# Value fetches issued behind the query and key fetches, and at the joint of two stages a product drawn forward, two sums per slice on GpSimd and a new order of blocks

## The chip, the cores and the metric

One core of a Trainium2 chip runs the whole kernel; the other cores are idle. The metric is the device time of one execution in microseconds (us), as the median over repeated executions. All data is float32. TensorE (PE in the profile) does the products, ScalarE (ACT) and VectorE (DVE) prepare their operands and take their results, GpSimd (POOL) does some sums and issues DMAs, SyncE (SP) only issues DMAs.

## The reference, cut to what matters

One layer of a bidirectional encoder over 512 tokens of width 1024: a half-step feed-forward, a mixer of two attentions (A and B) with gates, and a second half-step feed-forward.

```python
x = x + 0.5 * swiglu(rmsnorm(x, ffn1_norm), w1, w3, w2)       # FFN a
h = rmsnorm(x, mix_norm)
proj = h @ w_in                                               # A's q, k, v; B's q, k, v; gates
# A: 24 heads of 64 in 3 groups (dilation 1, 4, 16); banded scores with a table of biases,
scores = einsum(q, k) * 64 ** -0.5 + bias                     # masked outside the band
outs = softmax(scores) @ v                                    # groups joined by their log-sum-exp
merged = sigmoid(g_A) * (o_a @ w_branch_a) + sigmoid(g_B) * (o_b @ w_branch_b)
x = x + merged @ w_out
x = x + 0.5 * swiglu(rmsnorm(x, ffn2_norm), ...)              # FFN b
return rmsnorm(x, final_norm)
```

## The kernel before

Activations lie with features on the partitions: `x[0..7]`, eight tiles of 128 features by 512 tokens. Every float32 operand is split into a high part H and a rest L, and every product is three matmuls in a row (`mm3`, lines 256 to 258: H·H, H·L, L·H). A weight tile is fetched raw (`wr`, `wa`, `wt`), ScalarE makes its H (line 241) and VectorE its L (line 242).

PE's order is the order in which the code is written. The other engines' instructions are put in order by the framework, and each engine then works strictly in its order: a waiting instruction holds up all behind it, DMA issues included. DMAs are issued by SP and by GpSimd, each in its own queue.

**The joint of FFN a and the projection.** The last eight products of FFN a run over the rows of `x` in the order `ROWS = (0, 4, 1, 5, 2, 6, 3, 7)`. Behind each, `add` (lines 529 and 530, VectorE) updates `x[d]`, `norm_h` makes `hH[d]` on ScalarE (line 398) and `hL[d]` on VectorE (line 399), and `norm_sq` squares `x[d]` on ScalarE and adds it into `acc` (line 409; five of the adds on GpSimd, two on VectorE). From row pair k, `tq_steps` makes operands of a Strassen product: ScalarE copies the rows scaled into `Traw` (`put`), `sums` forms four sums of 128 x 256 on VectorE (lines 709 to 711), `part` splits them into `TH`, `TL` and `TQ` (line 718). PE's next product is the gate product g0 (`feat`), which takes `hH[k]`, `hL[k]` in the order k = 0..7. Behind it comes the Strassen projection of queries, keys and values (`project_qk`, slices f = 0, 2, .. 14, each of seven products A11, S1, S2, A12, S3, S4, A22 in the order that `slots` gives); for f = 0 the order is A11, A12, S1, ...; the S products read `TH`, `TL`, `TQ`.

**From the projection to the scores.** Finished slices are stored to DRAM by GpSimd: queries and keys to `qk_d` (line 746), values to `v_d` (line 762). `mixer` fetches them back: `fetch(0)` the six `qk` tiles of head pair 0, `fetch_v` the three value tiles `V0`, `V1`, `V2` of 1 MB each, all from GpSimd's queue. One gate product follows on PE (8 steps, `GAP_F`), then the scores of head pair 0 (`scores_a`): per step ("pair") 6 to 12 small matmuls into two PSUM banks (line 850), then two products of another gate block as a filler. VectorE adds the bias tile and takes the maximum (line 855); the bias tiles `W` (one per head) are fetched by SP from `zd`, each in two halves (lines 823 and 824); steps 0 and 1 need the first half only. There are four score banks, so step 2 waits until VectorE has read step 0's. After the four steps ScalarE takes exponentials, and their sums go through DRAM (`d`, lines 871 to 876) and come back in another order; SP then issues the `W` tiles of head pair 1. The tiles `qk` come from a ring of nine.

Of the kernel before, what the change touches and what calls it, by code (L numbers as in the profile page):

```python
# [25 lines left out]
NSW = NSQ + 6  # L26
ROWS = (0, 4, 1, 5, 2, 6, 3, 7)
# [13 lines left out]
NK = 8  # L41
# [28 lines left out]
def f32(t):  # L70
    return t.bitcast(F32)


class Layer:
# [56 lines left out]
    @staticmethod  # L131
    def slots(fs, ahead=False):
        at = {7 * i + 2 * j: (f, step) for i, f in enumerate(fs) for j, step in enumerate(STEPS)}
        if ahead:
            at[1] = at.pop(6)
        return [at[k] for k in sorted(at)]

    def ffn_order(self, s):
# [124 lines left out]
    def aux(self, name):  # L263
        return self.psa.tile([128, T], F32, tag="aux", name=name)

    def feat(self, name, n, done):
        ps = self.bank()
        H, L = self.weights(name, n)
        for k in range(NK):
            s = slice(128 * k, 128 * k + 128)  # L270
            self.mm3(ps, H[:, s], L[:, s], self.hH[k], self.hL[k], k == 0, k == NK - 1)
            if k == NK - 1:
                done(ps)
            yield

# [366 lines left out]
    def stream(self, items, held=None):  # L642
        nc = self.nc
        later = lambda fn: fn if held is None else lambda ps: held.append((fn, ps))
        for kind, n in items:
            if kind == "qk":
                hp, g = PAIRS[n]
                for part in range(2):

                    def done(ps, hp=hp, part=part, g=g):  # L650
                        t = self.qk[hp][part, g] = self.ap.tile([128, T], F32, tag="qk", name="qk", bufs=9)
                        nc.vector.tensor_mul(t.rearrange("p (r m) -> p r m", r=4),
                                             ps.rearrange("p (m r) -> p r m", r=4),
                                             self.acc.rearrange("p (r m) -> p r m", r=4))

                    yield from self.feat("waq", 2 * n + part, done)
            elif kind == "g":

                def done(ps, j=n):
                    z = self.tmp.tile([128, T], F32, tag="t", name="z")  # L660
                    nc.vector.tensor_mul(z, ps, self.R)
                    nc.sync.dma_start(self.gate_d[j], z)

                yield from self.feat("wg", n, later(done))
            elif kind == "pa":
                self.ma = [self.mp.tile([128, T], F32, name=f"ma{d}") for d in range(NK)]
                for d in range(NK):
                    ps = self.bank()
                    for k in range(4):
                        self.mm3(ps, *self.block("wpa", 4 * d + k), self.oH[k], self.oL[k], k == 0, k == 3)  # L670
                        if k == 3:
                            nc.scalar.copy(self.ma[d], ps)
                        yield
            else:
                toks = [(lambda t, i=i: t[:, 128 * i:128 * i + 128]) for i in range(4)]
                yield from self.token("wb", 4 * n, toks, lambda i, b, grp=n: self.rope(grp, i, b))
                self.turn()
            self.past.add((kind, n))

    def fetch(self, hp):  # L680
        for f, (h, g) in enumerate(PAIRS[:NSQ]):
            if h == hp:
                for part in range(2):
                    t = self.qk[hp][part, g] = self.ap.tile([128, T], F32, tag="qk", name="qk", bufs=9)
                    self.nc.gpsimd.dma_start(t, self.qk_d[2 * f + part])

    def fetch_v(self):
        for g in range(3):
            rows = self.v_d[g].rearrange("(m r) f -> m r f", r=4) if g else self.v_d[g].rearrange("(i p) f -> p i f", p=128)
            self.nc.gpsimd.dma_start(self.V[g], rows)  # L690

    def tq_open(self, gp):
# [5 lines left out]
    def tq_steps(self, k):  # L698
        nc = self.nc
        raw = self.cp.tile([128, 1024], F32, tag="c1", name="Traw").rearrange("p (c n) -> p c n", c=4)  # L700

        def put(e):
            d = k + 4 * e
            nc.scalar.activation(raw[:, 1:3] if e else raw[:, 0:4:3], self.x[d].rearrange("p (a n) -> p a n", a=2), AF.Copy,
                                 scale=self.par[:, G_MIX + d:G_MIX + d + 1])

        def sums():
            b = [raw[:, c] for c in (0, 3, 1, 2)]
            neg = lambda o, x, y: nc.vector.scalar_tensor_tensor(o, x, -1.0, y, op0=ALU.mult, op1=ALU.subtract)
            nc.vector.tensor_sub(b[0], b[0], b[1])  # L710
            nc.vector.tensor_sub(b[1], b[3], b[1])
            neg(b[3], b[3], b[0])
            neg(b[2], b[3], b[2])

        def part():
            for src, (H, L) in ((raw[:, 0:3], (self.TH[:, :, k], self.TL[:, :, k])), (raw[:, 3], (t[:, k] for t in self.TQ["S3"]))):
                nc.scalar.copy(H, src)
                nc.vector.tensor_sub(L, src, f32(H))

        return [lambda: put(0), lambda: put(1), sums, part]  # L720

    def project_qk(self, gp):
        nc, cp = self.nc, self.cp
        if True:
# [34 lines left out]

            def store_v(f, at, o):  # L760
                dst = self.v_d[(f - NSQ) // 2].rearrange("(i p) f -> p i f", p=128)
                nc.gpsimd.dma_start(dst[:, :, at:at + 256], o.rearrange("p (i f) -> p i f", i=4))

            def evict(f, step, ps):
                perm = f < NSQ and PAIRS[f][1] > 0
# [299 lines left out]
    def mixer(self):  # L1065
        nc, tc = self.nc, self.tc
# [4 lines left out]
        with tc.tile_pool(name="oA", bufs=1, reuse_waits="tile") as oa:  # L1071
            self.oH = [oa.tile([128, T], F32R, name=f"oH{h}") for h in range(4)]
            self.oL = [oa.tile([128, T], F32R, name=f"oL{h}") for h in range(4)]
            with tc.tile_pool(name="A", bufs=1, reuse_waits="tile") as ap:
                self.ap = ap
                self.V.append(ap.tile([128, 4, 512], F32, name="V2"))
                self.fetch(0)
                self.fetch_v()
                gap = lambda n: [next(fill) for _ in range(n)]
                gap(GAP_F)  # L1080
                held = None
                for hp in range(4):
                    if hp == 3:
                        self.until(fill, ("qk", 11))
                    res = []
                    self.weave(self.scores_a(hp, res), fill)
                    if hp < 3:
                        self.fetch(hp + 1)
                    if held:
                        gap(GAP_Y if hp > 1 else GAP_1)  # L1090
                        self.weave(self.values_a(hp - 1, *held), fill)
                    held = res
                gap(GAP_X)
                self.weave(self.values_a(3, *held), fill)
# [189 lines left out]
```

## Time and profile before

| | |
|---|---|
| time, median of 3 runs | 1277.19 us (1275.91 to 1277.29) |
| the profiled execution | 1272.24 us, of which the span of its instructions is 1270.5 us |
| TensorE busy | 1242.5 us, 98% of the span |
| VectorE, ScalarE, GpSimd busy | 917.2, 605.3, 131.2 us |
| mean granted TensorE clock | 0.992 |

A busy share is an average over the whole span. The times in the text are us from the first instruction of the profiled execution. Of the "joint" the text speaks for 322 to 364 us, of the "scores" for 505 to 560 us.

### The profile page before, as it was taken

The numbers are of one execution on the slowest core, as the hardware profiler recorded it, in microseconds if no ns is written. First come the engines' busy times: TensorE is split into PE (matmuls) and PEld (weight loads), VectorE is DVE, ScalarE is ACT, GpSimd is POOL, SyncE is SP. The second block draws the span as 40 slices with busy tenths as digits, with TensorE's granted clock in tenths as the row PEclk, the third lists the DMA queues.
The fourth block names the chain that finished last, engine by engine and source line by source line (L and its number), as shares of the span: only waits on it lengthen the run. The fifth ranks groups of instructions, "written<-read, shape, count | busy, mean of one in ns | idle before, by whom it ended". The sixth has DMA issues, their size and how long they took to land.

```text
span 1270.5 us, 20497 instructions
## 1 busy us (share of the span) xinstructions
PE 1242.5 (98%) x8214; PEld 1107.6 (87%) x8214; DVE 917.2 (72%) x1372; ACT 605.3 (48%) x903; POOL 131.2 (10%) x139
## 2 busy tenths in 40 slices
PE   9999999999999999699999999999999999999997
PEld 7897999899889999477788878888889989988996
DVE  7784687569988886366746798856777747874775
ACT  8551354155554445354423446655465415532553
POOL 1111110001212110310000200000301000100001
PEclk9999999999999999899999999999999999999998
DMA  9875766367369873853223220147837636743222
GB/s 299 232 187 177 189 187 181 98 168 198 100 147 258 249 200 113 302 168 102 76 104 108 83 92 26 34 142 215 223 101 199 183 94 176 194 150 106 62 82 67
DMA packets 88271, 192.95 MB, mean 152 GB/s; under 512 B 12768, under 2 KB 19312, under 8 KB 87920
## 3 DMA queue, kind: packets, MB, share of 16 engines
q1 hardware_dynamic: 68336, 142.32, 33.5%
q0 software_dynamic: 19120, 48.78, 18.3%
q8 instruction: 64, 1.05, 0.3%
q10 hardware_dynamic: 720, 0.55, 0.1%
q14 instruction: 31, 0.25, 0.1%
HBM read 176.84 MB, written 18.43 MB: 154 GB/s over the span
## 4 chain that ended last, share of the span: by engine, by line
PE 91%; DVE 4%; DMA 2%; issue 1%; ACT 1%; SPq 0%; POOL 0%; POOLq 0%; DVEq 0%
PE mm L256 23%; PE mm L257 22%; PE mm L258 22%; PE Y L257 4%; PE Y L256 4%; PE Y L258 4%; PE X L256 2%; PE X L257 2%; PE X L258 2%; PE S L850 1%; PE mm L901 1%; DMA qk<-qk_d 1%; PE Tb L1040 1%; PE T L919 1%; DVE wl L242 1%
## 5 line engine op out<-in xcount | busy, mean ns | idle before, releaser
L241 ACT CAST wh<-wr 128x1024 fp32r<-128x1024 f32 x133 | 139.4, 1049 | 178.4 <-PE mm L257 126.5
L256 PE MATMUL mm<-hH,wh 128*128 128x256 f32 (+1 forms) x600 | 201.4, 336 | 2.0 <-ACT hH L398 1.9
L257 PE MATMUL mm<-hL,wh 128*128 128x256 f32 (+1 forms) x600 | 196.6, 328 | 1.1 <-DVE hL L399 1.0
L258 PE MATMUL mm<-hH,wl 128*128 128x256 f32 (+1 forms) x600 | 196.4, 327 | 0.9 <-DVE wl L242 0.9
L242 DVE TENSOR_TENSOR wl<-wr,wh 128x1024 fp32r<-128x1024 f32 x133 | 163.0, 1226 | 29.3 <-ACT wh L241 28.9
L256 PE MATMUL mm<-gg,wh 128*128 128x512 f32 (+1 forms) x376 | 141.5, 376 | 0.0
L257 PE MATMUL mm<-gg,wh 128*128 128x512 f32 (+1 forms) x376 | 141.0, 375 | 0.0
L258 PE MATMUL mm<-gg,wl 128*128 128x512 f32 (+1 forms) x376 | 141.0, 375 | 0.0
L256 PEld LDWEIGHTS mm<-hH,wh 128*128 128x128 f32 x600 | 113.4, 189 | 17.9 <-issue 3.7
L257 PEld LDWEIGHTS mm<-hL,wh 128*128 128x128 f32 x600 | 113.6, 189 | 11.6 <-DVE hL L399 2.6
L258 PEld LDWEIGHTS mm<-hH,wl 128*128 128x128 f32 x600 | 113.2, 189 | 11.9 <-DVE wl L242 1.3
L257 PE MATMUL mm<-TL,wh 128*128 128x256 f32 x384 | 106.0, 276 | 0.0
L258 PE MATMUL mm<-TH,wl 128*128 128x256 f32 x384 | 106.0, 276 | 0.0
L256 PE MATMUL mm<-TH,wh 128*128 128x256 f32 x384 | 106.0, 276 | 0.0
L241 ACT CAST wh<-wa 128x1024 fp32r<-128x1024 f32 x54 | 56.8, 1051 | 96.0 <-PE mm L257 48.3
L241 ACT CAST wh<-ws 128x1024 fp32r<-128x1024 f32 x54 | 56.8, 1052 | 76.6 <-PE mm L257 49.2
L242 DVE TENSOR_TENSOR wl<-wt,wh 128x1024 fp32r<-128x1024 f32 x54 | 66.1, 1224 | 34.5 <-ACT wh L241 33.6
L529 DVE TENSOR_TENSOR u<-mm,R 128x512 f32<-128x512 f32 (+1 forms) x52 | 33.7, 648 | 79.2 <-PE mm L258 79.0
L241 ACT CAST wh<-wt 128x1024 fp32r<-128x1024 f32 x54 | 56.8, 1052 | 67.0 <-PE mm L257 39.8
L242 DVE TENSOR_TENSOR wl<-wa,wh 128x1024 fp32r<-128x1024 f32 x54 | 67.0, 1241 | 27.5 <-ACT wh L241 27.5
L256 PEld LDWEIGHTS mm<-gg,wh 128*128 128x128 f32 x376 | 70.6, 188 | 14.1 <-PE mm L258 0.9
L258 PEld LDWEIGHTS mm<-gg,wl 128*128 128x128 f32 x376 | 70.6, 188 | 12.9
(261 smaller groups left out, 3209.2 us busy)
## 6 DMA issues: line engine op xcount, KB each, us to landing
wr<-in_w2a SPq DMA_DIRECT2D x22, 512.0 KB, 3.7
wr<-in_w2b SPq DMA_DIRECT2D x22, 512.0 KB, 3.5
wt<-in_w13b SPq DMA_DIRECT2D x20, 512.0 KB, 4.1
wa<-in_w13b SPq DMA_DIRECT2D x20, 512.0 KB, 3.4
wt<-in_w13b POOLq DMA_DIRECT2D x20, 512.0 KB, 5.8
wt<-in_w13a SPq DMA_DIRECT2D x18, 512.0 KB, 3.5
wt<-in_w13a POOLq DMA_DIRECT2D x18, 512.0 KB, 6.0
wa<-in_w13a SPq DMA_DIRECT2D x18, 512.0 KB, 3.5
```

Of the source, the lines that this page charges most:

```text
L241: self.nc.scalar.copy(H, raw)
L242: self.nc.vector.tensor_sub(L, raw, f32(H))
L256: mm(out, lH, rH, start=start, stop=False, skip_group_check=more)
L257: mm(out, lH, rL, start=False, stop=False, skip_group_check=more)
L258: mm(out, lL, rH, start=False, stop=stop, skip_group_check=more)
L529: nc.vector.tensor_mul(u, ps, R)
L850: nc.tensor.matmul(*args, start=True, stop=True)
L901: nc.tensor.matmul(oc, v, p, start=st, stop=sp)
L919: nc.tensor.transpose(ps[:, 128 * b:128 * b + 128], P[h][:, c0 + 128 * b:c0 + 128 * b + 128], self.ident)
L1040: nc.tensor.transpose(pt[:, 128 * j:128 * j + 128], P[h, j][:, 128 * k:128 * k + 128], self.ident)
```

## The change

It has five parts: (1) `slots(..., ahead=True)` draws the A11 product of slice f = 2 in front of S1 of slice 0; (2) gate products take their blocks in the order `ROWS`; (3) for k = 0, 1, 2 the first two of the four sums of `sums` are made by GpSimd; (4) `fetch_v` is split: `V0` is issued behind the last `qk` fetch of head pair 0, `V1` and `V2` behind the third `qk` fetch of head pair 1; (5) the two value stores of the last slice (f = 14) are issued by SP.

```diff
     def slots(fs, ahead=False):
         at = {7 * i + 2 * j: (f, step) for i, f in enumerate(fs) for j, step in enumerate(STEPS)}
         if ahead:
-            at[1] = at.pop(6)
+            at[1], at[2], at[3] = at.pop(6), at.pop(7), at.pop(2)
...
-    def feat(self, name, n, done):
+    def feat(self, name, n, done, ks=range(NK)):
...
-        for k in range(NK):
+        for k in ks:
...
-                yield from self.feat("wg", n, later(done))
+                yield from self.feat("wg", n, later(done), ROWS)
...
-    def fetch_v(self):
-        for g in range(3):
-            rows = ...
+                    pins.append(self.nc.gpsimd.dma_start(t, self.qk_d[2 * f + part]))
+        return pins
+
+    def fetch_v(self, g, pin):
+        rows = ...
+        with self.tc.issue_after(pin.ins):
             self.nc.gpsimd.dma_start(self.V[g], rows)
...
-            nc.vector.tensor_sub(b[0], b[0], b[1])
-            nc.vector.tensor_sub(b[1], b[3], b[1])
+            eng = nc.gpsimd if k < 3 else nc.vector
+            eng.tensor_sub(b[0], b[0], b[1])
+            eng.tensor_sub(b[1], b[3], b[1])
             neg(b[3], b[3], b[0])
             neg(b[2], b[3], b[2])
...
-                nc.gpsimd.dma_start(dst[:, :, at:at + 256], o.rearrange("p (i f) -> p i f", i=4))
+                (nc.sync if f == NSW - 2 else nc.gpsimd).dma_start(dst[:, :, at:at + 256], ...)
...
-                self.fetch(0)
-                self.fetch_v()
+                self.fetch_v(0, self.fetch(0)[-1])
...
-                    if hp < 3:
-                        self.fetch(hp + 1)
+                    pins = self.fetch(hp + 1) if hp < 3 else []
+                    if hp == 0:
+                        self.fetch_v(1, pins[2])
+                        self.fetch_v(2, pins[2])
```

At the joint, GpSimd's rows in the changed kernel. `Traw_3275`, `Traw_3344` and `Traw_3417` are the sums' tiles of k = 0, 1, 2, and the `sq` tiles are the squares of rows 4, 1, 5, 2, 6:

```order
L409 TENSOR_TENSOR acc_93<-acc_93,sq_3271 128x512
L713 TENSOR_TENSOR Traw_3275<-Traw_3275 128x256
L714 TENSOR_TENSOR Traw_3275<-Traw_3275 128x256
L409 TENSOR_TENSOR acc_93<-acc_93,sq_3314 128x512
L713 TENSOR_TENSOR Traw_3344<-Traw_3344 128x256
L409 TENSOR_TENSOR acc_93<-acc_93,sq_3341 128x512
L714 TENSOR_TENSOR Traw_3344<-Traw_3344 128x256
L409 TENSOR_TENSOR acc_93<-acc_93,sq_3383 128x512
L713 TENSOR_TENSOR Traw_3417<-Traw_3417 128x256
L409 TENSOR_TENSOR acc_93<-acc_93,sq_3414 128x512
L714 TENSOR_TENSOR Traw_3417<-Traw_3417 128x256
```

Before, only the five `acc` rows stood there. The second sum (line 714) of k = 1 and of k = 2 stands behind one more `acc` add.

The same place on VectorE, from the update of row 3 to the update of row 7, before and then in the changed kernel; line 709 before and line 711 after are the two subtractions that read the sums:

```order
L529 TENSOR_TENSOR u_3451<-mm_3428,R_91 128x512
L711 TENSOR_TENSOR Traw_3417<-Traw_3417 128x256
L530 SCALAR_TENSOR_TENSOR x3_77<-u_3451,x3_77 128x512
L709 SCALAR_TENSOR_TENSOR Traw_3417<-Traw_3417 128x256
L718 TENSOR_TENSOR TQ_3274<-Traw_3417,TQ_3274 128x256
L709 SCALAR_TENSOR_TENSOR Traw_3417<-Traw_3417 128x256
L399 SCALAR_TENSOR_TENSOR hL3_108<-x3_77,par_82,hH3_100 128x512
L409 TENSOR_TENSOR acc_93<-acc_93,sq_3456 128x512
L718 TENSOR_TENSOR TL_187<-Traw_3417,TH_186 128x3x256
L529 TENSOR_TENSOR u_3478<-mm_3459,R_91 128x512
```

```order
L529 TENSOR_TENSOR u_3451<-mm_3428,R_91 128x512
L711 SCALAR_TENSOR_TENSOR Traw_3417<-Traw_3417 128x256
L721 TENSOR_TENSOR TQ_3274<-Traw_3417,TQ_3274 128x256
L711 SCALAR_TENSOR_TENSOR Traw_3417<-Traw_3417 128x256
L530 SCALAR_TENSOR_TENSOR x3_77<-u_3451,x3_77 128x512
L721 TENSOR_TENSOR TL_187<-Traw_3417,TH_186 128x3x256
L399 SCALAR_TENSOR_TENSOR hL3_108<-x3_77,par_82,hH3_100 128x512
L409 TENSOR_TENSOR acc_93<-acc_93,sq_3456 128x512
L529 TENSOR_TENSOR u_3478<-mm_3459,R_91 128x512
```

The VectorE sum of k = 2 is gone from here, and the update of `x3` now stands behind three rows that need GpSimd's sum.

Between projection and scores, the rows of GpSimd's queue before and then in the changed kernel. Tiles `qk_5421` to `qk_5431` belong to head pair 0, the others to head pair 1:

```order
L762 DMA v_d_115<-qo_5354 128x4x256
L690 DMA V0_5404<-v_d_115 128x4x512
L762 DMA v_d_115<-qo_5390 128x4x256
L690 DMA V1_5405<-v_d_115 128x2048
L685 DMA qk_5421<-qk_d_114 128x512
L685 DMA qk_5423<-qk_d_114 128x512
L685 DMA qk_5425<-qk_d_114 128x512
L685 DMA qk_5427<-qk_d_114 128x512
L685 DMA qk_5429<-qk_d_114 128x512
L685 DMA qk_5431<-qk_d_114 128x512
L690 DMA V2_5420<-v_d_115 128x2048
L685 DMA qk_5606<-qk_d_114 128x512
```

```order
L686 DMA qk_5429<-qk_d_114 128x512
L686 DMA qk_5431<-qk_d_114 128x512
L692 DMA V0_5404<-v_d_115 128x4x512
L686 DMA qk_5604<-qk_d_114 128x512
L686 DMA qk_5606<-qk_d_114 128x512
L686 DMA qk_5608<-qk_d_114 128x512
L686 DMA qk_5610<-qk_d_114 128x512
L686 DMA qk_5612<-qk_d_114 128x512
L692 DMA V1_5405<-v_d_115 128x2048
L692 DMA V2_5420<-v_d_115 128x2048
L686 DMA qk_5614<-qk_d_114 128x512
```

The six `qk` fetches of head pair 0 now stand directly behind the value store of slice 12, three `qk` fetches of head pair 1 stand behind `V0`, and `V1` and `V2` stand behind `qk_5612`.

SP's queue at the same place, before and then in the changed kernel (`W_5470` and `W_5473` before are `W_5468` and `W_5471` after, the bias tiles of the two heads of head pair 0):

```order
L208 DMA wr_5364<-in_waq 128x1024
L208 DMA wr_5441<-in_waq 128x1024
L662 DMA gate_d_113<-z_5467 128x512
L823 DMA W_5470<-zd_181 128x256
L824 DMA W_5470<-zd_181 128x2x128
L823 DMA W_5473<-zd_181 128x256
L824 DMA W_5473<-zd_181 128x2x128
L208 DMA wr_5500<-in_waq 128x1024
```

```order
L765 DMA v_d_115<-qo_5354 128x4x256
L208 DMA wr_5364<-in_waq 128x1024
L765 DMA v_d_115<-qo_5390 128x4x256
L208 DMA wr_5439<-in_waq 128x1024
L826 DMA W_5468<-zd_181 128x256
L827 DMA W_5468<-zd_181 128x2x128
L662 DMA gate_d_113<-z_5465 128x512
L826 DMA W_5471<-zd_181 128x256
L827 DMA W_5471<-zd_181 128x2x128
L208 DMA wr_5498<-in_waq 128x1024
```

The two value stores came in, the first head's `W` moved ahead of the store of the gate product, and the second head's `W` still stands behind it.

## Rows read from the trace of the kernel before

**Rows 1.** The page: busy time, share of the span and instructions of PE, and the shares by engine of the chain that ended last.
```profile
PE 1242.5 (98%) x8214; PEld 1107.6 (87%) x8214; DVE 917.2 (72%) x1372; ACT 605.3 (48%) x903; POOL 131.2 (10%) x139
PE 91%; DVE 4%; DMA 2%; issue 1%; ACT 1%; SPq 0%; POOL 0%; POOLq 0%; DVEq 0%
```

**Rows 2.** Waits of PE over the whole span: what waited, for what, us in total, times, the longest.
```profile
PE S L850 <- DMA qk<-qk_d: 11.4, 1, 11.4
PE mm L256 <- ACT hH L398: 1.9, 2, 1.0
PE S L850 <- DVE MX L855: 1.6, 2, 1.4
...
PE mm L257 <- DVE hL L399: 1.0, 2, 0.5
```

**Rows 3.** Stretches at the joint and in the scores: the stretch, its length, busy us (and instructions) of PE, PE's weight loads, DVE, ACT, POOL, the granted clock of PE, the busy share of the DMA engines, GB/s moved.
```profile
330.00:355.00 25.00, 22.66 (x97) 17.75 (x95) 25.00 (x38) 16.19 (x25) 6.03 (x4) 1.00 0.27 85
528.60:532.50 3.90, 3.86 (x12) 2.76 (x13) 1.11 (x5) 0.00 (x0) 0.54 (x1) 0.51 1.05 401
549.50:553.00 3.50, 3.50 (x13) 2.46 (x14) 1.98 (x12) 3.43 (x16) 0.00 (x0) 0.51 0.23 62
```

**Rows 4.** The timeline of PE at the end of the gate product g0: start, us, operation, idle time before it and what ended it.
```profile
354.65 0.50 PE L256 MATMUL mm<-hH,wh 128*128 128x512 f32 x1 [0.97 <-ACT hH L398]
355.69 0.50 PE L257 MATMUL mm<-hL,wh 128*128 128x512 f32 x1 [0.54 <-DVE hL L399]
```

**Rows 5.** The timeline of VectorE at the joint, with the same columns.
```profile
330.58 1.52 DVE L709 SCALAR_TENSOR_TENSOR Traw<-Traw 128x256 f32<-128x256 f32 x1
...
337.49 0.92 DVE L711 TENSOR_TENSOR Traw<-Traw 128x256 f32<-128x256 f32 x1
...
340.60 2.31 DVE L242 TENSOR_TENSOR wl<-wa,wh 128x1024 fp32r<-128x1024 f32 x1
...
344.31 0.41 DVE L710 TENSOR_TENSOR Traw<-Traw 128x256 f32<-128x256 f32 x1
344.64 0.68 DVE L530 SCALAR_TENSOR_TENSOR x<-u,x 128x512 f32<-128x512 f32 x1
345.24 1.21 DVE L242 TENSOR_TENSOR wl<-wa,wh 128x1024 fp32r<-128x1024 f32 x1
...
354.89 0.74 DVE L399 SCALAR_TENSOR_TENSOR hL<-x,par,hH 128x512 fp32r<-128x512 f32 x1
```

**Rows 6.** The timeline of GpSimd at the joint.
```profile
330.25 1.57 POOL L409 TENSOR_TENSOR acc<-acc,sq 128x512 f32<-128x512 f32 x1 [2.62 <-ACT sq L407]
336.59 1.54 POOL L409 TENSOR_TENSOR acc<-acc,sq 128x512 f32<-128x512 f32 x1 [4.77 <-ACT sq L407]
340.44 1.40 POOL L409 TENSOR_TENSOR acc<-acc,sq 128x512 f32<-128x512 f32 x1 [2.31 <-ACT sq L407]
346.75 1.53 POOL L409 TENSOR_TENSOR acc<-acc,sq 128x512 f32<-128x512 f32 x1 [4.92 <-ACT sq L407]
```

**Rows 7.** The timeline of PE in the scores: the first matmuls of head pair 0, its second step, the last filler of head pair 1 ahead of its third step, and that step.
```profile
528.64 2.08 PE L850 MATMUL S<-qk 64*128 64x256 f32 x8 [11.38 <-DMA qk<-qk_d]
...
533.05 1.08 PE L850 MATMUL S<-qk 64*128 64x256 f32 x12
...
535.66 0.60 PE L850 MATMUL S<-qk 64*128 64x128 f32 x6
...
545.93 0.40 PE L258 MATMUL mm<-hH,wl 128*128 128x512 f32 x1
547.73 0.49 PE L850 MATMUL S<-qk 64*128 64x128 f32 x2 [1.40 <-DVE MX L855]
```

**Rows 8.** The timeline of GpSimd's DMA issues ahead of the scores.
```profile
511.20 0.75 POOL L762 DMA_DIRECT2D v_d<-qo  x1 [8.55 <-ACT qo L758]
512.09 0.75 POOL L690 DMA_DIRECT2D V<-v_d  x1
...
513.75 0.55 POOL L690 DMA_DIRECT2D V<-v_d  x1
514.85 2.15 POOL L685 DMA_DIRECT2D qk<-qk_d  x4 [0.55 <-DMA wr<-in_waq]
```

**Rows 9.** The timeline of SP's DMA issues in the scores.
```profile
518.02 0.33 SPq L662 DMA_DIRECT2D gate_d<-z  x1
518.44 0.75 SPq L823 DMA_DIRECT2D W<-zd  x1
...
541.43 0.38 SPq L823 DMA_DIRECT2D W<-zd  x1
```

**Rows 10.** The bias tiles `W` in the stretch 515 to 550: time from issue to landing, least, median and longest.
```profile
DMA to landing us min/median/max: 4.7/7.2/12.2
```

**Rows 11.** The timeline of VectorE at the first step of head pair 0 (second head) and at the first step of head pair 1.
```profile
532.17 0.42 DVE L855 CUSTOM_DVE_ANT_0 P<-S,W 128x256 f32<-128x256 f32 x1 [0.67 <-DMA W<-zd]
...
546.90 0.43 DVE L855 CUSTOM_DVE_ANT_0 P<-S,W 128x256 f32<-128x256 f32 x1 [3.71 <-DMA W<-zd]
```

**Rows 12.** Stretches of 5 us ahead of and in PE's wait, columns as in rows 3.
```profile
510.00:515.00 5.00, 5.00 (x31) 4.42 (x30) 3.33 (x4) 1.96 (x4) 2.96 (x5) 1.00 0.46 132
515.00:520.00 5.00, 2.26 (x10) 1.53 (x9) 1.92 (x2) 1.04 (x1) 2.53 (x5) 1.00 1.02 337
520.00:525.00 5.00, 0.00 (x0) 0.00 (x0) 0.00 (x0) 0.00 (x0) 1.07 (x2) 0.72 1.02 414
```

More of the change, by code (lines that the diff above doesn't have):

```diff
@@ L264, in aux @@
         return self.psa.tile([128, T], F32, tag="aux", name=name)
-    def feat(self, name, n, done):
+    def feat(self, name, n, done, ks=range(NK)):
         ps = self.bank()
         H, L = self.weights(name, n)
-        for k in range(NK):
+        for k in ks:
             s = slice(128 * k, 128 * k + 128)
-            self.mm3(ps, H[:, s], L[:, s], self.hH[k], self.hL[k], k == 0, k == NK - 1)
-            if k == NK - 1:
+            self.mm3(ps, H[:, s], L[:, s], self.hH[k], self.hL[k], k == ks[0], k == ks[-1])
+            if k == ks[-1]:
                 done(ps)
@@ L680, in fetch @@
     def fetch(self, hp):
+        pins = []
         for f, (h, g) in enumerate(PAIRS[:NSQ]):
@@ L684, in fetch @@
                     t = self.qk[hp][part, g] = self.ap.tile([128, T], F32, tag="qk", name="qk", bufs=9)
-                    self.nc.gpsimd.dma_start(t, self.qk_d[2 * f + part])
-    def fetch_v(self):
-        for g in range(3):
-            rows = self.v_d[g].rearrange("(m r) f -> m r f", r=4) if g else self.v_d[g].rearrange("(i p) f -> p i f", p=128)
+                    pins.append(self.nc.gpsimd.dma_start(t, self.qk_d[2 * f + part]))
+        return pins
+    def fetch_v(self, g, pin):
+        rows = self.v_d[g].rearrange("(m r) f -> m r f", r=4) if g else self.v_d[g].rearrange("(i p) f -> p i f", p=128)
+        with self.tc.issue_after(pin.ins):
             self.nc.gpsimd.dma_start(self.V[g], rows)
@@ L761, in store_v @@
                 dst = self.v_d[(f - NSQ) // 2].rearrange("(i p) f -> p i f", p=128)
-                nc.gpsimd.dma_start(dst[:, :, at:at + 256], o.rearrange("p (i f) -> p i f", i=4))
+                (nc.sync if f == NSW - 2 else nc.gpsimd).dma_start(dst[:, :, at:at + 256], o.rearrange("p (i f) -> p i f", i=4))
             def evict(f, step, ps):
```

## The prediction, made before the result was known

> **What bounds the kernel now.** I read the page first: PE is busy for 98% of the span and makes up 91% of the chain that ended last [rows 1]. So a microsecond counts only where PE stands still or runs slowly, and the list of PE's waits is the next view. It is short [rows 2]: 11.4 us once for `qk` tiles from DRAM, 1.9 and 1.0 us for `hH` and `hL` in the gate product at the joint, 1.6 us for VectorE's maximum `MX` in the scores. The change touches these two places.
>
> *Scores.* PE's first score matmul starts at 528.64 after 11.38 us without work, so PE was free at 517.26 [rows 7]. Behind that the granted clock is 0.51 from 528.60 to 532.50, which is the lower level, 1.2 of 2.4 GHz [rows 3]. Step 0 with its two filler products lasts from 528.64 to 533.05 = 4.41 us, the next such stretch 533.05 to 535.66 = 2.61 [rows 7]; the slow clock costs 1.8 us. In head pair 1 the last filler matmul starts at 545.93, a matmul of this size takes about 0.23 us of PE's time, and the third step begins at 547.73 [rows 7]: 1.6 us lost. From 549.50 to 553.00 the clock is 0.51 again [rows 3]: 3.5 x 0.49 = 1.7 us. Together 11.4 + 1.8 + 1.6 + 1.7 = 16.5 us could be had here at most.
>
> *Joint.* VectorE is busy for 25.00 of the 25.00 us from 330 to 355 [rows 3]; PE waits at the last block of g0 for `hH7` (0.97) and `hL7` (0.54) [rows 4]. VectorE's queue sets that end: `hL7` starts at 354.89 [rows 5] and PE goes on at 355.69.
>
> **The change part by part.**
>
> *Order of the blocks.* `hH[3]` and `hH[7]` are the late ones in the old order; in the new one only block 7, the last, can make PE wait. But the end of g0 is `hL7` plus two matmuls either way. Alone it is worth 0: the earlier wait is had at block 7.
>
> *A11 drawn forward.* It puts 24 matmuls between A12 and S1, as cover if `TH` is late. The waits of PE [rows 2] show no wait of S1 for `TH`, so there is nothing to cover: 0. If the sums get later, it hides up to 24 x 0.115 = 2.8 us at S1 (a matmul of half the size at half of 0.23).
>
> *Sums on GpSimd.* Six rows leave VectorE. One holds it for 344.31 to 344.64 = 0.33 us [rows 5], so 6 x 0.33 = 2.0 us less. What GpSimd's six rows cost VectorE has to be bounded. GpSimd's adds of 128 x 512 take 1.40 to 1.57 us [rows 6]; a sum has half the elements, an estimated 0.70 to 0.79. While such an add runs, the VectorE rows that read two SBUF tiles stretch: at 330.58 a subtraction takes 1.52 us instead of 0.41 and ends 0.28 us after GpSimd's add (330.25 + 1.57 = 331.82); at 340.60 a weight row takes 2.31 instead of 1.21; at 337.49 a sum takes 0.92 instead of 0.41 [rows 5, 6]. So an add costs VectorE 0.5 to 1.1 us. A sum of half the size costs 0.25 (half of the smallest) to 0.79 (all of it): six cost 1.5 to 4.7 us. I take 0.45 each, 2.7, since about a third of the rows around read PSUM (`u`) and are not held. Net so far +0.7.
>
> The Trainium skill says, in "SBUF — State Buffer", section "SBUF: two separate sides", that VectorE with two SBUF inputs and GpSimd share one port pair as an exclusive lock for a whole instruction. The stretched rows agree with it; by the rule alone every sum would hold VectorE for its full length, the upper end above.
>
> To that comes waiting in order. VectorE's two subtractions and the rows behind them (for k = 2 the update of `x3`, then `hL3`) now stand behind GpSimd's second sum, which for k = 1 and 2 stands behind one more `acc` add. The add at 346.75 ends at 348.28 [rows 6]; with a sum behind it that is about 349.0, and VectorE used the sum of k = 2 from about 347.6, having made it itself: up to 1.4 us idle. For k = 1 the add at 336.59 ends at 338.13, the sum at 338.9, about when VectorE came to it: 0. I take 1.3 in all. Joint: 0.7 + 1.3 = **+2.0 us**, bounds -2.0 (no hold, no wait) to +4.7 - 2.0 + 1.4 = +4.1.
>
> *Fetch of queries and keys first.* In the old queue `V0` and `V1` (1 MB each) are issued at 512.09 and 513.75, ahead of `qk` from 514.85 on, and the queue stood still 8.55 us before 511.20 for a value store of slice 14 [rows 8]. In the new queue that store is not there: the `qk` fetches can go out from about 502.7 on, when that standstill began. The six are 1.5 MB; at the 337 GB/s of the stretch from 515 [rows 12] that is 4.5 us, so even with some us of waiting for free tiles they land by about 512, ahead of 517.3. The 11.4 us wait for `qk` goes. If the fetches were still held to 514.85 as the first one is now, they would land near 520 and PE would wait 2.7 us.
>
> *What is late next: the bias tiles.* VectorE's first step needs `W` of both heads. The second head's `W` is issued by SP behind the gate store at 518.02 [rows 9], which waits for PE's gate product, so about 518.4 to 518.9 in either kernel. Today it lands just before 532.17, and VectorE waits 0.67 us for it [rows 11]; this is hidden behind the wait for `qk`. From there a chain runs that PE cannot shorten: maximum, exponentials, sums out to DRAM and back, `W` of head pair 1 issued at 541.43 [rows 9], VectorE at 546.90 [rows 11], PE's third step at 547.73: 15.6 us from 532.17. So with X the time at which the second `W` is there, PE reaches that step at X + 15.6, and not before 517.26 + (546.16 - 528.64 - 1.8) = 533.0, its own work. X would have to be 517.4 for no loss, before the issue. The gain is therefore 532.17 - X, as long as X is later than that.
>
> X: the shortest landing of a `W` here takes 4.7 us, the longest 12.2 [rows 10]: 518.5 + 4.7 = 523.2 to 530.7. By bytes: ahead of it from 511 on are on SP two value stores, two weight tiles (0.5 MB each), the first head's `W` and the gate store (0.25 each) and 0.13 of its own, and beside it `V0` and three `qk` (1.75): 4.4 MB. The stretches move 132 GB/s while the queues fill, then 337 and 414 [rows 12]: 0.7 MB by 515, 2.3 by 520, the remaining 2.1 at 414 in 5.0 us, 525.0. `V1` and `V2` come only behind `qk_5612`, whose predecessor needs a tile that PE gives back with step 1 (about 521), so their first bytes come near 524 and touch only the end. I take X = 525.7, a little over the sum: **gain 6.5 us**. The two slow-clock stretches I leave as they are: the standstill is only divided in two (about 3 us at step 2 of head pair 0, 5 at head pair 1); the first stretch lies in the chain's slack.
>
> By the Trainium skill, "DMA: Bandwidth & Descriptors", section "Queues, rings and completion order", each DMA engine goes round its queues packet by packet. In that case `V1`'s large packets beside `W`'s small ones would bring X near the upper end, 530.7; no row here separates this from the byte count, and the rival below prices it.
>
> *Value stores on SP.* 1 MB more ahead of `W` in its queue, counted above. `V0` to `V2` are needed after 560, so fetching them later costs nothing.
>
> **Sum.** -6.5 + 2.0 = -4.5 us. The profiled execution took 1272.24 us, 1.74 more than its span, and would take 1267.7; it stands 5.0 below the median of the runs, 1277.19, so on the median **1272.7 us**. About 0.2%, 2.5 us, is what a measurement can tell from no change.
>
> **The rivals.**
>
> *Clean gain.* X at its lower bound, 523.2, and a joint without holding (-1): -9.0 - 1.0 = -10, about 1267; with the round trip of the sums through DRAM less disturbed (the last 5.4 us of the chain are a landing whose least is 4.7 and whose start also waited) up to -13, 1264. For it: SP's queue is empty of `V1` and `V2` when `W` goes. Against: 1 MB of stores ahead of it. Chance 0.2.
>
> *`W` takes the place of `qk`.* X = 530: gain 2.2, joint +2: -0.2, about 1277, no change. For it: 12.2 us landings beside the same `V1` and `V2` now. Chance 0.17.
>
> *Slower: `W` lands later than now.* Two value stores, written to DRAM in small pieces, stand ahead of it in SP's queue and share the DMA engines with `V0`, then `V1` and `V2`. From X = 532.7 on the loss at the joint is no longer paid for by 2.5 us less; at X = 535 it is 2.8 + 2.0 = +4.8, 1282. Against: less stands before it in bytes than now. Chance 0.13.
>
> *Sums without effect.* If VectorE's end at the joint does not move (GpSimd's sums cost as much as they save), the forecast is 6.5 less, 1270.7; it lies inside the first case.
>
> **How the numbers follow.** My forecast (gain from 2.5 to 9) has 0.5, its own range is 1268 to 1275. Faster by over 0.2%: 0.5 + 0.2 less a little for their edges, 0.67; within 0.2%: 0.19; slower: 0.14. Leaving out about 1 in 10 at each end gives 1265 to 1279.5.
>
> **What would show it.** Right: the list of PE's waits has no `qk`, but `MX` with 6 to 9 us in two or three pieces in the scores; VectorE's first step waits for `W` until about 526; at the joint VectorE rows beside GpSimd's sums are stretched, `hL7` starts near 357 and PE's wait there grows to about 6 us in all. Wrong: `hL7` not later than 354.9 (sums free), the second `W` there before 523 or after 530, or `qk` still in the list.

## The result, and the profile after

The changed kernel is slower: 1281.03 us (median of 11 runs, 1278.75 to 1285.20) against 1275.91 (11 runs, 1271.97 to 1277.83), a ratio of 1.0050 with a 95% interval of 1.0036 to 1.0065. Its profiled execution has a span of 1278.6 us, 8.1 more than before.

The page's first line and the first line of the chain, which answer to [rows 1]: PE is busy for about as long as before, in a longer span, and DMA's share of the chain has doubled.

```profile
PE 1246.5 (97%) x8214; PEld 1110.6 (87%) x8214; DVE 916.6 (72%) x1366; ACT 605.0 (47%) x903; POOL 135.8 (11%) x143
PE 88%; DMA 4%; DVE 4%; ACT 2%; issue 1%; POOL 0%; SPq 0%; POOLq 0%; DVEq 0%; ACTq 0%
```

The waits of PE, which answer to [rows 2] (lines 853 and 858 are 850 and 855 of the kernel before):

```profile
PE S L853 <- DVE MX L858: 12.7, 4, 4.4
PE mm L256 <- ACT hH L398: 4.4, 2, 2.7
PE mm L256 <- ACT c L778: 1.6, 1, 1.6
```

The `qk` wait of 11.4 us is gone, as forecast. In its place stand 12.7 us of waiting for VectorE's maxima (1.6 before), the `hH` wait at the joint is 4.4 instead of 1.9, and a wait for a copy `c` of ScalarE is new.

The joint, PE's timeline (start, us, operation, idle before it and what ended it). PE's last wait for an `hH` in g0 ends at 357.94, 3.3 us later than in [rows 4]; at 377.74 comes the new wait, in S3, the fifth product of slice 0:

```profile
354.01 0.50 PE L256 MATMUL mm<-hH,wh 128*128 128x512 f32 x1 [2.74 <-ACT hH L398]
...
357.94 0.79 PE L256 MATMUL mm<-hH,wh 128*128 128x512 f32 x1 [1.68 <-ACT hH L398]
...
377.74 0.38 PE L256 MATMUL mm<-TQ,wh 128*128 128x256 f32 x1 [1.55 <-ACT c L778]
```

VectorE at the joint, its three waits for a sum of GpSimd (in a timeline row "x2" counts rows put together), the update of `x3`, and `hL7`, which answers to the last row of [rows 5]:

```profile
329.83 0.88 DVE L711 SCALAR_TENSOR_TENSOR Traw<-Traw 128x256 f32<-128x256 f32 x2 [1.44 <-POOL Traw L714]
...
340.99 0.43 DVE L711 SCALAR_TENSOR_TENSOR Traw<-Traw 128x256 f32<-128x256 f32 x1 [0.63 <-POOL Traw L714]
...
351.22 0.43 DVE L711 SCALAR_TENSOR_TENSOR Traw<-Traw 128x256 f32<-128x256 f32 x1 [1.28 <-POOL Traw L714]
...
352.33 0.68 DVE L530 SCALAR_TENSOR_TENSOR x<-u,x 128x512 f32<-128x512 f32 x1
...
358.18 0.74 DVE L399 SCALAR_TENSOR_TENSOR hL<-x,par,hH 128x512 fp32r<-128x512 f32 x1
```

`hL7` starts 3.3 us later than at 354.89 (3.1 if counted from the first matmul of g0, which starts at 346.99 instead of 346.77), and VectorE stood idle for 1.44 + 0.63 + 1.28 = 3.35 us for the sums. The wait at 351.22 is the one seen in the order: GpSimd's `acc` add stands ahead of the sum, and that add had itself waited for ScalarE's square. GpSimd's timeline there:

```profile
348.96 1.52 POOL L409 TENSOR_TENSOR acc<-acc,sq 128x512 f32<-128x512 f32 x1 [4.04 <-ACT sq L407]
350.45 0.73 POOL L714 TENSOR_TENSOR Traw<-Traw 128x256 f32<-128x256 f32 x1
```

The scores. PE's timeline at the third step of head pair 0 and of head pair 1, and VectorE's waits behind them:

```profile
532.89 0.79 PE L853 MATMUL S<-qk 64*128 64x128 f32 x2 [3.73 <-DVE MX L858]
538.09 2.07 PE L853 MATMUL S<-qk 64*128 64x128 f32 x14 [4.41 <-DVE MX L858]
...
552.45 0.49 PE L853 MATMUL S<-qk 64*128 64x128 f32 x2 [1.54 <-DVE MX L858]
555.94 2.07 PE L853 MATMUL S<-qk 64*128 64x128 f32 x14 [3.01 <-DVE MX L858]
```

```profile
532.06 0.42 DVE L858 CUSTOM_DVE_ANT_0 P<-S,W 128x256 f32<-128x256 f32 x1 [5.99 <-DMA W<-zd]
537.26 0.42 DVE L858 CUSTOM_DVE_ANT_0 P<-S,W 128x256 f32<-128x256 f32 x1 [4.42 <-DMA W<-zd]
```

PE reaches the scores at 523.85 without a wait, and VectorE then waits for `W` of the first head until 532.06 and of the second until 537.26. SP issued the second at 525.09; its first half was there 12 us later. Three stretches show the low clock (columns as in [rows 3]): behind the wait at the joint, in the wait at head pair 0, and behind that at head pair 1:

```profile
354.00:360.00 6.00, 3.53 (x6) 1.80 (x7) 5.97 (x11) 4.07 (x7) 0.00 (x0) 0.59 0.00 0
536.00:540.00 4.00, 1.91 (x14) 1.78 (x14) 2.37 (x15) 1.68 (x2) 0.00 (x0) 0.50 0.97 392
556.00:560.00 4.00, 4.00 (x19) 3.39 (x20) 3.00 (x19) 3.87 (x17) 0.00 (x0) 0.51 0.24 64
```

Before, the clock at the joint stayed at 1.00, in the stretch of [rows 3] and in the one behind it:

```profile
355.00:360.00 5.00, 4.46 (x37) 4.22 (x37) 4.80 (x9) 3.85 (x6) 1.06 (x1) 1.00 0.32 105
```

### The profile page after: what moved, and what is told of

The parts are those of the page before. It is cut to its first block, busy times and chain, and to the rows that moved or that the text cites. A ratio compares the mean times of both kernels' runs of the same rounds, so it can differ in the third digit from the quotient of the medians.

```text
span 1278.6 us, 20505 instructions
## 1 busy us (share of the span) xinstructions
PE 1246.5 (97%) x8214; PEld 1110.6 (87%) x8214; DVE 916.6 (72%) x1366; ACT 605.0 (47%) x903; POOL 135.8 (11%) x143
## 4 chain that ended last, share of the span: by engine, by line
PE 88%; DMA 4%; DVE 4%; ACT 2%; issue 1%; POOL 0%; SPq 0%; POOLq 0%; DVEq 0%; ACTq 0%
PE mm L256 22%; PE mm L258 21%; PE mm L257 21%; PE Y L256 4%; PE Y L257 4%; PE Y L258 4%; PE X L256 2%; PE X L257 2%; PE X L258 2%; DMA wt<-in_w13b 2%; DMA W<-zd 1%; PE mm L904 1%; PE Tb L1043 1%; PE T L922 1%; PE S L853 1%
```

## The experiments

All ratios are to the kernel before, run beside each; its median there was 1275.35 to 1276.14 us. "PE late by" compares the start of the same PE instruction in the profiled executions. "PE's stretch" is the time from the start of the first matmul of g0 to the start of the last one ahead of the scores: 170.1 us in the kernel before (346.77 to 516.87), and 170.1 to 170.2 in three runs that leave the joint as it was (e3, e10, e11). First each half alone, then the edits at the joint one by one, then the scores.

**The joint alone** (e15). The kernel before with the edits (1), (2), (3).

```diff
-            at[1] = at.pop(6)
+            at[1], at[2], at[3] = at.pop(6), at.pop(7), at.pop(2)
...
-                yield from self.feat("wg", n, later(done))
+                yield from self.feat("wg", n, later(done), ROWS)
...
+            eng = nc.gpsimd if k < 3 else nc.vector
+            eng.tensor_sub(b[0], b[0], b[1])
+            eng.tensor_sub(b[1], b[3], b[1])
```

> The kernel before with only the three edits at the joint (sums on GpSimd, order of blocks, A11 drawn forward), fetches and stores as before. Theory (joint and scores add up; in the changed kernel PE is 6.3 us late behind the first Strassen products and 6.6 at the first score product): PE 6 to 7 us late ahead of the scores, the qk wait 11 us as before, the time about 1282.5, 6.4 above the kernel before. Rival (the scores take back part of a late start, as they are bound by transfers): under 1280.

Measured: 1282.52 us, ratio 1.0055 (1.0033 to 1.0076), 6.5 above the kernel before. PE's waits, `qk` among them as before:

```profile
PE S L853 <- DMA qk<-qk_d: 11.0, 1, 11.0
PE mm L256 <- ACT hH L398: 6.2, 3, 2.7
PE S L853 <- DVE MX L858: 3.8, 2, 2.5
PE mm L256 <- ACT c L778: 1.6, 1, 1.6
```

PE's stretch is 6.9 us longer than before (347.92 to 524.91). The joint's edits cost 6.5 us where the forecast had 2.0.

**The fetches alone** (e3). The kernel before with edits (4) and (5).

```diff
-                self.fetch(0)
-                self.fetch_v()
+                self.fetch_v(0, self.fetch(0)[-1])
...
+                    if hp == 0:
+                        self.fetch_v(1, pins[2])
+                        self.fetch_v(2, pins[2])
...
-                nc.gpsimd.dma_start(dst...
+                (nc.sync if f == NSW - 2 else nc.gpsimd).dma_start(dst...
```

> The kernel before with only the new order of the fetches and the two value stores on SP. Theory (the second head's bias tile W takes the place of qk: it lands 12 to 13 us after the gate store, PE waits for it at step 2 of head pair 0 and of head pair 1): no qk wait, 8 us of MX waits in head pair 0 and 4 in head pair 1, low clock twice, the time 0 to 2 us above the kernel before. Rival (the forecast's sum was right for the scores and only the joint was mis-sized): the second W lands near 526, the time is 5 to 7 us below the kernel before.

Measured: 1277.14 us, ratio 1.0010 (0.9997 to 1.0023): no change. VectorE's waits for the two heads' `W`, and the traffic of the two queues from 527 to 533 (q1 is SP's, q0 GpSimd's: packets, MB, share of the DMA engines' time):

```profile
526.93 0.42 DVE L858 CUSTOM_DVE_ANT_0 P<-S,W 128x256 f32<-128x256 f32 x1 [6.80 <-DMA W<-zd]
534.16 0.42 DVE L858 CUSTOM_DVE_ANT_0 P<-S,W 128x256 f32<-128x256 f32 x1 [6.46 <-DMA W<-zd]
```

```profile
q0 software_dynamic: 315, 2.15, 86.1%
q1 hardware_dynamic: 280, 0.38, 17.2%
```

With both queues busy each moves about as many packets, but GpSimd's (`V1`, `V2`, `qk`) hold 6.8 KB on the average and SP's (`W`, weights, the gate store) 1.4 KB: SP's queue gets 15% of the bytes. Earlier in the same run, from 520 to 522, GpSimd's packets (`V0`, `qk`) hold 3.4 KB; the counts are about equal again, and SP's queue gets 23% of the bytes. From 524 to 526 GpSimd's queue is nearly empty, and SP's moves 0.72 MB in 2 us:

```profile
q0 software_dynamic: 184, 0.62, 76.0%
q1 hardware_dynamic: 189, 0.19, 27.2%
...
q1 hardware_dynamic: 635, 0.72, 99.6%
q0 software_dynamic: 17, 0.06, 7.5%
```

The second `W`, issued at 519.10, is there at 534.1, 2 us later than in the kernel before. An 11.4 us wait has been exchanged for one of 4.5 + 6.4.

**The sums back on VectorE** (e1), all else as changed.

```diff
-            eng = nc.gpsimd if k < 3 else nc.vector
+            eng = nc.vector
```

> The changed kernel with all four sums of every k on VectorE again, the rest as changed. Theory (the six GpSimd sums hold VectorE and make it wait, so that g0's end comes 4.5 us late and PE's clock falls): the end of g0 returns to within 0.5 us of the kernel before (hL7 near 355), the low clock at 354 to 360 is gone, the time falls by 4 to 5 us from the changed kernel's 1281, to about 1276.5. Rival (the block order or the product drawn forward causes the late end): hL7 stays near 358 and the time near 1281.

Measured: 1280.36 us, ratio 1.0035 (1.0021 to 1.0048), 0.7 below the changed kernel. At the joint the theory holds: `hL7` starts at 355.16 instead of 358.18 and PE leaves g0 3.0 us earlier. The low clock did not go, though: PE has one wait of 2.92 us there, and behind it the clock of the stretch 355 to 360 is 0.66. The time did not follow either: PE came to the scores at 520.91, 2.9 us earlier, and VectorE had the second `W` at 538.04, 0.8 later than in the changed kernel:

```profile
538.04 0.42 DVE L858 CUSTOM_DVE_ANT_0 P<-S,W 128x256 f32<-128x256 f32 x1 [5.01 <-DMA W<-zd]
```

So the 3 us were lost again in waiting for it.

**A11 back at its old place** (e2), all else as changed.

```diff
-            at[1], at[2], at[3] = at.pop(6), at.pop(7), at.pop(2)
+            at[1] = at.pop(6)
```

> The changed kernel with A11 of slice 2 back at its old place. Theory (drawn forward, A11 leaves S2 and S3 of slice 0 next to each other on one PSUM bank, and PE waits 1.6 us for ScalarE's copy c at 376): this wait is gone, S1 does not wait for TH, the time falls by 1.5 to 2 us to about 1279.2. Rival (A11 covers late TH and TL after the sums got later): S1 waits up to 2.7 us and the time does not fall.

Measured: 1281.62 us, ratio 1.0045 (1.0029 to 1.0061). The wait for `c` is gone, S1 does not wait for `TH`, PE is at the scores 1.6 us earlier (522.21 against 523.85); but the time is that of the changed kernel, as with the sums: PE waits 15.6 us for `MX` there instead of 12.7:

```profile
PE S L853 <- DVE MX L858: 15.6, 4, 6.2
```

The mechanism holds, the expected gain does not.

**Only A11 drawn forward** (e17), in the kernel before.

> The kernel before with only A11 of slice 2 drawn in front of S1 of slice 0. Theory (S2 and S3 of slice 0 then stand next to each other on one PSUM bank, PE waits 1.6 us for ScalarE's copy between them): that wait of 1.5 to 1.6 us shows near 372, PE is 1.8 us late behind it, and the time about 1277.5, 1.8 above the kernel before. Rival (the wait comes only with the late joint): no such wait, no change.

Measured: 1277.14 us, ratio 1.0010 (0.9998 to 1.0022), and the wait in PE's timeline:

```profile
373.68 0.38 PE L256 MATMUL mm<-TQ,wh 128*128 128x256 f32 x1 [1.55 <-ACT c L775]
```

It comes without a late joint, and PE's stretch is 2.0 us longer (347.32 to 519.46). The time agrees with +1.8 us and cannot be told from nothing.

**Only the sums on GpSimd** (e14), in the kernel before.

> The kernel before with only the six sums on GpSimd. Theory (they hold VectorE and make it wait in order): hL7 starts 3 us later than 354.9, PE leaves g0 3 to 4.5 us later than before, all the rest shifted by that. Rival (the sums hurt only with the other order of blocks): under 1.5 us.

Measured: a single execution, 1279.27 us. `hL7` at 358.55, PE 3.7 us late at the end of g0, its stretch 3.2 us longer (347.39 to 520.68), the three waits of VectorE for the sums together 3.3 us as in the changed kernel. PE's wait in g0 with the old order of blocks is one long one, for the `hH` of row 3, whose update stands behind GpSimd's sum of k = 2; the clock behind it (355 to 360) is 0.70:

```profile
354.38 0.61 PE L256 MATMUL mm<-hH,wh 128*128 128x512 f32 x1 [4.74 <-ACT hH L398]
```

**Only the order of blocks** (e13, e16), in the kernel before; run twice.

> The kernel before with only the blocks of the gate products in the order of rows. Theory (the end of g0 is set by hL7, so the order alone is worth nothing; PE's two waits become one of about 2.9 us): PE leaves g0 within 0.5 us of before and the clock stays at its upper level. Rival (the one longer wait lets the clock fall, as in e1_sums_back, where PE was 0.8 us later after it): PE 0.8 to 1.5 us late behind g0.

> e13_rows_only once more, timed: the kernel before with only the blocks of the gate products in the order of rows. Theory (one wait of 2.9 us instead of four shorter ones lets the clock fall to its lower level behind it, most times): low clock at 355 to 360 again, PE 1 to 2.5 us late, the time 1 to 3 us above the kernel before. Rival (the low clock of the one look was chance, as in one other run here without this order): no low clock, no change.

Measured: a single execution at 1278.79 us; then 1275.33 us, ratio 1.0006 (0.9993 to 1.0018). Each profile shows one wait for an `hH`, that of row 7, instead of two, 2.91 us the first time and 2.30 the second, and the low clock behind it (355 to 360: the first, then the second run):

```profile
355.00:360.00 5.00, 4.63 (x17) 3.93 (x18) 4.83 (x8) 3.29 (x6) 0.52 (x1) 0.50 0.33 105
```

```profile
355.00:360.00 5.00, 4.46 (x23) 4.21 (x23) 4.76 (x8) 2.72 (x5) 1.13 (x1) 0.66 0.33 105
```

PE's stretch is 2.5 us longer in the first (347.25 to 519.84) and 1.1 in the second (347.28 to 518.43). In the time this does not show, so a cost in the time is not shown. The low clock stood behind g0 in all nine runs with this order; but in e9, with the old order, it stood there too (0.66), behind waits of 0.35, 0.41, 0.97 and 0.54 us, so the merged wait is not the only thing it can follow.

**`W` of head pair 0 on GpSimd** (e7), behind the six `qk`, all else as changed.

```diff
+                self.fetch(0)
+                self.W0 = self.fetch_w(0, self.nc.gpsimd)
+                self.fetch_v(0, self.wpin)
-                self.fetch_v(0, self.fetch(0)[-1])
...
```

`fetch_w` is the old code of the four `W` fetches, with the issuing queue as an argument.

> The changed kernel with the two bias tiles W of head pair 0 issued by GpSimd directly behind the six qk fetches, ahead of V0; all else as changed. Theory (W's place in SP's queue behind the stores and beside V0 to V2 is what holds the scores): W lands by about 523, no MX wait in head pair 0, the chain to head pair 1 starts 12 us earlier, the time falls by 10 to 15 us from the changed kernel, to about 1268. Rival (the DMA engines are simply full from 515 to 540 and something else lands late in its place): the gain is under 3 us.

Measured: 1278.08 us, ratio 1.0024 (1.0011 to 1.0038): 3 us below the changed kernel, far from the 10 to 15. `W`'s first halves land at 522.05 and 522.81, but VectorE's first step starts no earlier:

```profile
532.71 0.42 DVE L863 CUSTOM_DVE_ANT_0 P<-S,W 128x256 f32<-128x256 f32 x1 [5.07 <-DMA v_d<-qo]
```

It now waits for the second value store of slice 14, issued at 520.27 and landed at 532.55: `P` lies where that store reads from. The store is late as `W` was before: it goes through SP's queue, which shares the engines with `V0` and `qk`. That is the rival's mechanism, and its bound of 3 us fits.

**`V0` later too** (e9), fetch edits alone.

```diff
-                self.fetch_v(0, self.fetch(0)[-1])
+                self.fetch(0)
...
-                        self.fetch_v(1, pins[2])
-                        self.fetch_v(2, pins[2])
+                        for g in range(3):
+                            self.fetch_v(g, pins[3])
```

> As e3_scores_only (the kernel before with the new fetch order and the stores on SP), but V0 too is fetched behind a qk tile of head pair 1 that waits for PE's step 1 of head pair 0 (about 521), as V1 and V2 then are. Theory (V0 beside SP's queue is what makes the second value store and W land late: 524.8 and about 533 in e3): the second store lands by 521, the second W by 527, the MX waits in head pair 0 fall from 11 us to about 4, the time is 4 to 8 us below e3's 1277. Rival (the stores are slow by themselves, in 1 KB pieces, whatever runs beside them): the second store lands at 524 again and the time stays near 1277.

Measured: 1270.52 us, ratio 0.9961 (0.9947 to 0.9974), 5.5 below the kernel before. The second store lands at 522.15 (524.76 with `V0` beside it), VectorE has the second `W` at 525.35. What is left is a wait at head pair 1:

```profile
523.96 0.43 DVE L858 CUSTOM_DVE_ANT_0 P<-S,W 128x256 f32<-128x256 f32 x1 [3.59 <-DMA W<-zd]
...
543.34 0.42 DVE L858 CUSTOM_DVE_ANT_0 P<-S,W 128x256 f32<-128x256 f32 x1 [6.63 <-DMA W<-zd]
```

**`V0` later and `W` on GpSimd** (e10), fetch edits alone.

> As e9_scores_v_late, with W of head pair 0 issued by GpSimd directly behind the six qk tiles. Theory (the late W is the only thing between the removed qk wait and the gain forecast for it): no wait over 1 us in head pair 0, the round trip of the sums starts about 10 us earlier than in the kernel before, the time is 8 to 13 us below the kernel before, near 1265. Rival (VectorE's P tiles lie where the value stores read from, so VectorE waits for the second store whatever W does; in e7_w_gpsimd it waited for it until 532.7): a wait for a store of 3 us or more stands in the place of W's, gain 3 to 6 us.

Measured: 1270.37 us, ratio 0.9961 (0.9941 to 0.9981). Both were half right: the first head pair waits 2.55 us for the store and PE hardly (0.56), but the time stays: at head pair 1 PE waits 5.74 + 4.14 us. SP's issues show why; the stores of the sums into `d` (6 KB and twice 1 KB, in pieces of 16 B) are issued from 529.24 on, and the `SO` that reads them back can go only at 539.21:

```profile
529.24 0.38 SPq L879 DMA_DIRECT2D d<-SO  x1
529.66 1.16 SPq L881 DMA_DIRECT2D d<-SO  x2
531.00 0.49 SPq L826 DMA_DIRECT2D W<-zd  x1
539.21 0.33 SPq L883 DMA_DIRECT2D SO<-d  x1
```

`V1`, `V2` and `qk` of head pair 2 land between 533 and 540 beside it. From 533 to 536 SP's packets are the pieces of 16 B, and the two queues again move about as many:

```profile
q0 software_dynamic: 250, 1.20, 97.0%
q1 hardware_dynamic: 257, 0.00, 4.8%
```

From 530 to 532 the trace has no packet of SP's queue; what held the stores until then is not shown.

**`V1` and `V2` behind head pair 1** (e11), on top of e10.

```diff
                     if hp == 0:
-                        for g in range(3):
-                            self.fetch_v(g, pins[3])
+                        self.fetch_v(0, pins[3])
+                    elif hp == 1:
+                        self.fetch_v(1, pins[5])
+                        self.fetch_v(2, pins[5])
```

> As e10_scores_w_v_late, with V1 and V2 fetched behind the last qk tile of head pair 2, which waits for PE's last step of head pair 1, V0 as in e10. Theory (in e10 the store of the sums, 1 KB each, took 9 us beside V1 and V2, and PE's 10 us of waiting at head pair 1 are this): the stores of the sums land within 3 us, the MX waits at head pair 1 fall from 9.9 us to 2 to 5, the time falls by 5 to 8 us to about 1264, 11 below the kernel before. Rival (the round trip of the sums is long by itself, whatever moves beside it, or V1 and V2 now come late for the values): the time stays at 1270.

Measured: 1266.98 us, ratio 0.9939 (0.9922 to 0.9956): the fastest kernel here, 8.4 us below the kernel before and 14 below the changed one. The stores of the sums land at 534.71, PE waits at head pair 1 for 5.3 us in all instead of 9.9:

```profile
PE S L858 <- DVE MX L863: 6.1, 3, 4.3
```

The theory's direction holds; of its 11 us 8.4 came. The step from e10 to e11, 3.4 us, is little more than the noise: the two intervals overlap a little.

**The joint's edits in front of these scores** (e18, e19), with the sums on GpSimd and without.

> The changed kernel whole, its joint too, with the fetches of e11_w_v_later (W of head pair 0 on GpSimd behind the six qk, V0 behind PE's step 1 of head pair 0, V1 and V2 behind head pair 1). Theory (the joint's 6.5 us of e15_joint_only are PE time that is lost wherever the scores do not wait for transfers anyway): e11's 1267.0 plus 6 to 6.5, about 1273.3. Rival (the scores take back a late start, as undoing the sums or the drawn product in the changed kernel won nothing): 1267 to 1270.

> As e18_all_w_v_later with all four sums on VectorE. Theory (in e1_sums_back the 3 us won at the joint were lost again only because the second W there landed at the same time whenever PE came): now they count, the time is 2.5 to 3.5 us below e18_all_w_v_later. Rival (the sums cost nothing in the time): equal within 1 us.

Measured: 1273.50 us (ratio 0.9988, 0.9978 to 0.9998) and 1269.36 (0.9947, 0.9932 to 0.9962). The joint costs 6.5 us here too, the sums 4.1 of them, A11 and the order of blocks the other 2.4, and PE's `MX` waits are the same 6.1 and 6.2 us as without the joint's edits. So the joint's loss is PE time, and it counts where `W` is not late. In the changed kernel undoing the sums or A11 won nothing because VectorE had the second `W` no earlier (538.04 and 538.55 against 537.26), though its gate store was issued 2.9 and 1.6 us earlier; why it came no earlier is not shown.

## Why the prediction was wrong, point by point

**The `qk` wait.** Right: it went, and the fetches landed in time (the last at 520.62, PE needed it at 523.85). They were issued later than I had them, from 509.30 and, five of them, from 513.19 on. Most of that is the late joint: in e3 it was 503.36 and 507.25, against 502.7 in the forecast, and PE's first score matmul came at 517.90 without a wait.

**The time X of the second `W`**: this term was mis-sized, the gain of 6.5 us with it. I had 525.7, 7.7 us behind the gate store at 518.02; in the kernel with the fetch edits alone (e3) it was 534.1, 15.4 behind a gate store at 518.73. The chain behind X held: 15.6 us to PE's third step of head pair 1 in the forecast, 15.4 in e3 (549.60) and 15.2 in the changed kernel (552.45).

The step that failed is the byte count: it shared the DMA engines by bytes, so that 4.4 MB ahead of `W` would be through by 525, and it let `V1` and `V2` "touch only the end". They were issued about when I had them (523.05 and 525.38 in e3), but beside them the end took 8 us. In the run each queue got about one packet in turn, and SP's are the small ones. SP's share is then set by GpSimd's packet size, and the queue that holds `W` moves at 0.06 MB/us (0.38 MB in 6 us) of some 0.4. The rule of the Trainium skill that I cited for X near 530.7 ("DMA: Bandwidth & Descriptors", section "Queues, rings and completion order"), that each DMA engine goes round its queues packet by packet, was the better forecast; 315 packets against 280 agree with it.

I wrote that no row separates this rule from the byte count. None that I had chosen does, but the trace of the kernel before does, in the view of its two queues from 527 to 533:

```profile
q0 software_dynamic: 463, 2.06, 88.7%
q1 hardware_dynamic: 462, 0.29, 15.8%
```

The counts are equal there, and SP's queue gets 12% of the bytes. With `V0` out of the way (e9) X is 525.35. That this is my figure is chance, since my sum had `V0` in it; it shows that what made `W` late was not the bytes ahead in SP's own queue, but what moved beside it.

I also took the longest landing in the kernel before, 12.2 us, as a bound [rows 10]. It was no bound: with two value stores ahead, 14.8 us came out.

**The joint: +2.0 forecast, +6.5 measured**, outside the bound of +4.1. Three terms failed.

The sums, forecast +2.0, delay `hL7` by 3.1 us in the changed kernel and by 3.0 alone (e14), counted from the first matmul of g0. The waiting in order was forecast at 1.3 and is 3.35: for k = 2 I had up to 1.4 (measured 1.28), but 0 for k = 1 (0.63), and k = 0 (1.44) does not stand in my sum at all, though both its sums stand behind an `acc` add. The rest, forecast at +0.7 (2.7 of holding less 2.0 of work), is about 0: 3.1 less 3.35. The sums themselves take 0.73 us where nothing holds them, as estimated.

A11 drawn forward, forecast 0, costs 1.6 us of PE's time in the changed kernel (against e2) and 2.0 alone (e17). I had asked only whether what it moves ahead of is late, and not what it had kept apart: it stood between S2 and S3 of slice 0, which use one PSUM bank with ScalarE's copy between them. The order of PE's queue would have shown this; the orders that I had set out were those of GpSimd, VectorE and SP.

The order of blocks, forecast 0, makes, with the sums on VectorE, one wait for `hH` of 2.3 to 2.9 us out of two pairs of shorter waits (0.96 and 0.41, 0.97 and 0.54). The clock was low behind it in all runs with this order, and stayed up in the kernel before and in e3, e10, e11 and e17, with the old order and the sums on VectorE; in one such run (e9) it fell as well, and PE's stretch there is about 1 us longer. The order's cost, 1.1 and 2.5 us of PE's stretch, does not show in the time of that edit alone.

In PE's time the three add up: 3.2 for the sums, 2.0 for A11 and 1.1 to 2.5 for the order make 6.3 to 7.7, and the joint alone (e15) has 6.9.

**Sum.** The two halves alone give +6.5 and +1.0 (the second cannot be told from nothing), together 7.5; the changed kernel is 5.1 slower, since its scores wait for `W` and hide part of the late joint: the second `W` is there at 537.26 instead of 532.17, which is 5.1 later.

**The rivals.** "`W` takes the place of `qk`" (0.17) named the mechanism of the scores, with X = 530. "Slower" (0.13) came true, but not by its mechanism alone: `W` was 2 us later than before in the fetch edits alone, as it said from 532.7 on, and the larger part was the joint. Of the signs that I gave for being wrong, the second `W` after 530 came true.

## What to carry to other kernels

When two DMA queues shared the engines here, the small pieces in one went at the packet rate of the other: count packets in turn, not bytes, and issue large prefetches only when no small transfer on a chain (here bias tiles and 1 KB round trips) is under way. A removed wait is worth the distance to the next late operand, so find that one's landing in the new traffic before crediting anything. Work moved to another engine must be read in that engine's order too, and an instruction moved forward leaves a gap behind: look at which neighbours it had kept apart.

## What the runs showed that I had not expected

- Two queues with work shared by packets: 315 to 280 packets, 2.15 to 0.38 MB from 527 to 533 in the run with the fetch edits alone, and 250 to 257 from 533 to 536 in e10, where SP's packets held 16 B.
- Stores of 1 KB and 6 KB in pieces of 16 B took 10 us in all (529.24 to 539.19) beside packets of 4 and 8 KB, and 5.5 (529.17 to 534.71) with `V1` and `V2` out of the way.
- PE's clock fell to its lower level behind a single wait of 2.3 us (0.66 over 355 to 360), while pairs of waits of 0.96 + 0.41 and 0.97 + 0.54 us, 4 to 5 us apart, left it up in the five runs that had them; in e9, with 0.35 in place of 0.96, it fell too.
- A GpSimd sum of 128 x 256 took 0.73 us alone and 1.18 to 1.19 in three of six cases, beside VectorE rows with two SBUF operands (0.92 in a fourth): holding goes both ways.
